# A hybrid block on one core: where half of a convolution is computed, and how attention's operands are split

## The chip, the cores and the metric

The kernel runs on one core of one Trainium2 chip. The metric is the time of one execution on the device in microseconds (us), the median of several runs. The engines go by the profile's names: PE is TensorE's matmul side and PEld its weight loads, DVE is VectorE, ACT is ScalarE, POOL is GpSimd, SP is SyncE, which here issues nearly all DMAs.

## The reference

One decoder layer for 1024 positions of 1024 channels in float32. Of it, what matters here:

```
h = rmsnorm(x);  proj = h @ w_in             # 13320 columns, split into branches
(ml_q.. ml_f, sc_b, sc_c, sc_u, sb_q, sb_k, sb_v, g_ml, g_sc, g_sb) = split(proj)
y_ml = mLSTM mixer of ml_*                   # 4 heads of 256
y_sc = sc_b * causal_conv3(sc_c * sc_u)      # per channel, 1024 channels
# stick-breaking attention, 16 heads of 64, strictly causal:
z = q k^T / 8;  a[t,s] = sigmoid(z_ts) * prod_{s<j<t} (1 - sigmoid(z_tj));  y_sb = a v
merged = sum over branches of sigmoid(g) * (y @ w_proj)
x = x + merged @ w_out;  x = x + relu(rmsnorm(x) @ w_up)^2 @ w_down;  rmsnorm(x)
```

## The kernel before, in words

**Precision.** Each float32 operand is split in two: hi, the value rounded to the matmul type float32r (ScalarE), and lo, the rest (VectorE). `split` does that (L135). A product takes three matmuls, hi by hi, hi by lo and lo by hi (`mm3`, L130 to L133).

**Stages in order of time.** The norm and transpose of x (to 100 us); the mLSTM mixer (to some 530 us); attention (537 to 1275 us); the rest of the projections of h as products of seven (to 1500 us); the three branch projections; the output projection; the MLP.

**Plain projection and product of seven.** `dense_ws` (L160) computes 128 columns of h @ w_in, transposed: two halves of 512 positions, each 8 row blocks times 3 matmuls of 128 x 512, so 48. `unit` (L781) computes 256 columns for all 1024 positions by a scheme for 2 x 2 blocks with seven products instead of eight: 7 x 4 x 3 = 84 matmuls of 128 x 512. The sums of its weight blocks are made on GpSimd (`left`, L647), and its outputs are added together on VectorE (L807).

**The convolution branch.** `sc_unit` (L693) gives three plain projections for one tile of 128 channels, and its evacuations multiply, shift and add on VectorE (L707 to L717). `conv_units` (L813) does two tiles of channels with three units. `NSC` says how many of the eight tiles go the first way; before it is 8, so the loop over `conv_units` (L836) is empty.

**Attention.** The loop over p (L748) takes 8 head pairs. `sb_v` (L497) projects v for two head pairs at once into 8 buffers, the last positions first; these are all the buffers of that kind, so the next `sb_v` waits until attention has read them. `sb_qk` (L509) projects k and q. q and k have 64 channels per head, so hi and lo of one head are stacked in 128 partitions, and two matmuls give all four products (L557, L558: one stack of q against k's stack, and against the stack with its halves swapped). Before, ScalarE and VectorE write halves of 64 partitions, and four copies by DMA (L531 to L534) fill the second halves of k's four stacks. The rings hold 6 stacks of q and 10 of k, of which a head pair uses 4 and 8.

`sb_attn` (L542) goes through blocks G of 256 queries from the last to the first, each with two heads hh. For each of two query tiles it goes through chunks of up to 512 keys from the right: scores (L557, L558), two sigmoids on ScalarE (L560, L561), masks on GpSimd for the diagonal block (L565, L567), a running product from right to left on VectorE (L573) that starts from the last value of the chunk before it (copied by L571), and a product on GpSimd (L574). The result is transposed (L591), split (L594 to L597), and multiplied with v (L604 to L608), where v's hi and lo stand side by side and so come out in the two halves of the partitions. The last diagonal block, which only the second query tile uses, has its hi and lo side by side in one matmul of 256 columns (L604) into columns 256 to 511 of the accumulator. L614 and L615 add the halves of the partitions over all 512 columns, and L618 adds the columns of that block, twice.

**What sets the order.** The order of each engine's instructions is fixed when the kernel is built: a scheduler walks through a simulated time line and lets each engine take the ready instruction with the lowest priority number, which is the order of writing. `tc.high_priority(offset=AHEAD)` puts attention 2000 places ahead, so projections fill the time that attention leaves. The projections for the convolution stand behind attention's code in each turn of the loop, three per head pair (L756), ahead of the next `sb_qk`. Two banks of PSUM (`acc`) serve all projections of this stage.

**Behind attention** the gates follow: for each of three branches, four units with a sigmoid, whose results go to DRAM (`sg_d`, L838 to L846).

Of the kernel before, what the change touches and what calls it, by code (L numbers as in the profile page):

```python
# [16 lines left out]
P = 128  # L17
# [15 lines left out]
N_RAW, N_HI, N_LO, N_SM = 2, 5, 5, 160  # L33
GROUPS = ((0, 1), (2, 3), (4, 5, 6, 7))
AHEAD = 2000
NSC = 8


@with_exitstack
def hybrid_block_kernel(  # L40
# [66 lines left out]
    def g(name):  # L107
        return rings[name].get()
# [5 lines left out]
    def unplan(base, *names):  # L114
        base.absorb(*[rings.pop(n) for n in names])
# [9 lines left out]
    def f32(ap):  # L125
        return ap.bitcast(F32)
# [382 lines left out]
    def sb_qk(p):  # L509
        Q = [[None, None], [None, None]]  # L510
        T = [[None, None] for _ in range(4)]

        def ev_q(th, ps):
            a, b = g("Q"), g("Q")
            A, B = slice(0, 64), slice(64, 128)
            r = slice(0, 512)
            nc.scalar.activation(a[A, r], ps[A, :], AF.Copy)
            nc.scalar.activation(b[B, r], ps[B, :], AF.Copy)
            nc.vector.tensor_tensor(a[B, r], ps[A, :], f32(a[A, r]), ALU.subtract)
            nc.vector.tensor_tensor(b[A, r], ps[B, :], f32(b[B, r]), ALU.subtract)  # L520
            Q[0][th], Q[1][th] = a, b

        def ev_k(th, ps):
            t1, t2, t3, t4 = [g("T") for i in range(4)]
            A, B = slice(0, 64), slice(64, 128)
            r = slice(0, 512)
            nc.scalar.activation(t1[A, r], ps[A, :], AF.Copy)
            nc.scalar.activation(t2[B, r], ps[B, :], AF.Copy)
            nc.vector.tensor_tensor(t3[A, r], ps[A, :], f32(t1[A, r]), ALU.subtract)
            nc.vector.tensor_tensor(t4[B, r], ps[B, :], f32(t2[B, r]), ALU.subtract)  # L530
            nc.sync.dma_start(f32(t1[B, r]), f32(t3[A, r]))  # L531
            nc.sync.dma_start(f32(t3[B, r]), f32(t1[A, r]))
            nc.sync.dma_start(f32(t2[A, r]), f32(t4[B, r]))
            nc.sync.dma_start(f32(t4[A, r]), f32(t2[B, r]))  # L534
            for i, t in enumerate((t1, t2, t3, t4)):
                T[i][th] = t

        dense_ws(w_in, C_SBK + p * P, hT, ev_k)
        dense_ws(w_in, C_SBQ + p * P, hT, ev_q)
        return Q, T  # L540

    def sb_attn(p, Q, T, vt):  # L542
        for G in range(3, -1, -1):
            yo = g("yo")
            for hh in range(2):
                kx, ky = (T[0], T[2]) if hh == 0 else (T[1], T[3])
                ga = {}
                for ti in (1, 0):
                    Tt = 2 * G + ti
                    qs = Q[hh][Tt // 4][:, (Tt % 4) * P:(Tt % 4 + 1) * P]  # L550
                    n = (Tt + 1) * P
                    nch = (n + 511) // 512
                    prev = None
                    for ch in range(nch - 1, -1, -1):
                        w = min(512, n - ch * 512)
                        ps = g("z")
                        mm(ps[:, :w], qs, kx[ch][:, :w], start=True, stop=False)  # L557
                        mm(ps[:, :w], qs, ky[ch][:, :w], start=False, stop=True)  # L558
                        u, be = g("u"), g("be")
                        nc.scalar.activation(u[:, :w], ps[:, :w], AF.Sigmoid, scale=-0.125)  # L560
                        nc.scalar.activation(be[:, :w], ps[:, :w], AF.Sigmoid, scale=0.125)  # L561
                        free(ps)
                        if prev is None:
                            dg = slice(w - P, w)
                            nc.gpsimd.affine_select(out=u[:, dg], in_=u[:, dg], compare_op=ALU.is_gt, fill=1.0,  # L565
                                                    base=0, pattern=[[-1, P]], channel_multiplier=1)
                            nc.gpsimd.affine_select(out=be[:, dg], in_=be[:, dg], compare_op=ALU.is_gt, fill=0.0,  # L567
                                                    base=0, pattern=[[-1, P]], channel_multiplier=1)
                            nc.gpsimd.memset(u[:, w:w + 1], 1.0)
                        else:  # L570
                            nc.gpsimd.tensor_copy(u[:, w:w + 1], prev[:, 0:1])  # L571
                        ur = u[:, 0:w][:, ::-1]
                        nc.vector.tensor_tensor_scan(ur, ur, ur, u[:, w:w + 1], ALU.mult, ALU.bypass)  # L573
                        nc.gpsimd.tensor_tensor(be[:, :w], be[:, :w], u[:, 1:w + 1], ALU.mult)  # L574
                        if prev is not None:
                            free(prev)
                        prev = u
                        ga[ti, ch] = be
                    free(prev)
                pav = g("av")  # L580
                ns = 2 * G + 2
                last = 1 if G else 0
                for s2 in range(G, -1, -1):
                    pt = g("tp")
                    for k in (0, 1):
                        s = 2 * s2 + k
                        for ti in (0, 1):
                            if s == ns - 1 and ti == 0:
                                continue
                            blk = ga[ti, s // 4][:, (s % 4) * P:(s % 4 + 1) * P]  # L590
                            nc.tensor.transpose(pt[:, k * 256 + ti * P:k * 256 + (ti + 1) * P], blk, ident)  # L591
                    ah, al = g("ah"), g("ah")
                    if s2 == G:
                        split(ah[:, 0:256], al[:, 0:256], pt[:, 0:256])  # L594
                        split(ah[:, 256:384], ah[:, 384:512], pt[:, 384:512])
                    else:
                        split(ah[:, 0:512], al[:, 0:512], pt)  # L597
                    free(pt)
                    for k in ((1, 0) if s2 == G else (0, 1)):
                        s = 2 * s2 + k  # L600
                        hd = 2 * (p % 2) + hh
                        vs = vt[s][:, hd * P:(hd + 1) * P]
                        if s == ns - 1:
                            mm(pav[:, 256:512], vs, ah[:, 256:512], start=True, stop=True)  # L604
                            continue
                        o = slice(k * 256, (k + 1) * 256)
                        mm(pav[:, 0:256], vs, ah[:, o], start=(s == ns - 2), stop=False)  # L607
                        mm(pav[:, 0:256], vs, al[:, o], start=False, stop=(s == last))  # L608
                    free(ah, al)
                free(*ga.values())  # L610
                tmp = g("avt")
                hi_r = slice(0, 64) if hh == 0 else slice(64, 128)
                lo_r = slice(64, 128) if hh == 0 else slice(0, 64)
                nc.scalar.activation(tmp[hi_r, 0:512], pav[lo_r, :], AF.Copy)  # L614
                nc.vector.tensor_tensor(yo[hi_r, 0:512], pav[hi_r, :], tmp[hi_r, 0:512], ALU.add)  # L615
                free(pav, tmp)
            for o in (256, 384):
                nc.vector.tensor_tensor(yo[:, 128:256], yo[:, 128:256], yo[:, o:o + P], ALU.add)  # L618
            nc.sync.dma_start(ysb_d[p][:, G * 256:(G + 1) * 256], yo[:, 0:256])
            free(yo)  # L620
            if G == 2:
                free(*[t[1] for t in Q + T])
        free(*[t[0] for t in Q + T])
# [124 lines left out]
    for p in range(8):  # L748
        if p % 2 == 0:
            vt = sb_v(p // 2)  # L750
        Q, T = sb_qk(p)
        with tc.high_priority(offset=AHEAD):
            sb_attn(p, Q, T, vt)
        if p % 2 == 1:
            free(*vt[::-1])
        for c0, ev in conv[len(conv) * p // 8:len(conv) * (p + 1) // 8]:  # L756
            dense_ws(w_in, c0, hT, ev)
    unplan(ring_r, "Q", "T", "V", "ah")
    unplan(ring_f, "u", "be", "yo", "avt", "sc")
    unplan(banks, "z", "av", "acc", "tp")  # L760
# [75 lines left out]
    for ct in range(NSC, KO, 2):  # L836
        conv_units(ct)
    for b, c0 in enumerate((C_GML, C_GSC, C_GSB)):  # L838
        for ct in range(0, KO, 2):
            sg = unit(c0 + ct * P, 0, AF.Sigmoid)  # L840
            for n, th in ((0, 0), (1, 1), (0, 1), (1, 0)):
                v = sg[n][th][:, :512]
                if (n, th) != (1, 0):
                    nc.scalar.activation(v, v, AF.Sigmoid)
                nc.sync.dma_start(sg_d[b][ct + n][th], v)
            free(*sg[0], *sg[1])  # L846
# [384 lines left out]
```

## Time and profile before

| | |
|---|---|
| median of three runs | 2516.52 us (2516.36 to 2519.3) |
| the profiled execution's own time | 2517.91 us |
| its span | 2516.2 us |
| mean granted clock of TensorE | 0.991 |
| busy, PE / DVE / ACT / POOL | 2449.4 / 1600.2 / 1166.7 / 870.8 us |
| matmuls | 12648 |
| chain of waits, share of PE | 87% |

A busy time is the union of an engine's instructions. A slice row cuts the span into 40 equal parts and gives the busy share of each in tenths. A window row gives the busy time of each engine in one stretch. Matmuls overlap in the records (one of 512 columns shows some 0.39 us while the next starts 0.23 us after it), so the rate is counted from starts. The chain of waits is followed backwards from the last instruction, each step to what released it.

### The profile page before, as it was taken

Reading aid. Unit: us, or ns where it says so; the run is one execution under the profiler, and the core shown is the slowest. Engines: PE = TensorE matmul, PEld = TensorE weight load, DVE = VectorE, ACT = ScalarE, POOL = GpSimd, SP = SyncE. Lnnn points to the kernel's source line nnn. Section 1 sums busy time; section 2 is a strip of 40 time slices with the busy share of each in tenths; the row PEclk is TensorE's granted clock in tenths of the full one; section 3 lists DMA queues with packets and bytes.
Section 4 is the critical chain, followed back from the end, with each engine's and each line's share of the span. In section 5 each row is a group of like instructions: output and inputs, shape, how many; then the busy total and the mean of one; then the engine's idle time right before and its main releaser. Section 6 shows DMA issues by size and latency. Waiting matters only on the chain.

```text
span 2516.2 us, 35640 instructions
## 1 busy us (share of the span) xinstructions
PE 2449.4 (97%) x12648; PEld 2064.5 (82%) x12648; DVE 1600.2 (64%) x2425; ACT 1166.7 (46%) x2358; POOL 870.8 (35%) x1188
## 2 busy tenths in 40 slices
PE   7999999999999999999899999999989999899998
PEld 6899998988888888988678878888868888678876
DVE  6564554667757757767853352444366777788896
ACT  5443333346546546546554451212456666643343
POOL 6500000024424434434732200000246565654563
PEclk9999999999999999999999999999999999999999
DMA  4321211122122122122243482433326665865663
GB/s 135 102 64 34 68 47 51 39 72 66 32 72 66 35 70 65 35 74 70 86 147 101 126 275 79 132 93 106 132 80 201 205 201 185 279 236 190 232 208 127
DMA packets 295914, 290.26 MB, mean 115 GB/s; under 512 B 22832, under 2 KB 227632, under 8 KB 295736
## 3 DMA queue, kind: packets, MB, share of 16 engines
q1 hardware_dynamic: 293288, 283.53, 36.1%
q10 hardware_dynamic: 2448, 4.46, 0.5%
q8 instruction: 99, 1.62, 0.3%
q14 instruction: 79, 0.65, 0.1%
HBM read 195.63 MB, written 83.90 MB: 111 GB/s over the span
## 4 chain that ended last, share of the span: by engine, by line
PE 87%; DVE 5%; POOL 3%; issue 2%; ACT 2%; DMA 2%; SPq 0%; POOLq 0%; ACTq 0%; DVEq 0%
PE ps L131 27%; PE ps L132 27%; PE ps L133 26%; PE ps L591 2%; DVE gr L138 2%; PE ps L558 1%; PE ps L557 1%; PE ps L608 1%; PE ps L607 1%; POOL gf L645 1%; DVE gf L573 1%; POOL gf L574 1%; DVE gf L1186 1%; DMA gf<-in_x_dram 0%; DVE wl L138 0%
## 5 line engine op out<-in xcount | busy, mean ns | idle before, releaser
L131 PE MATMUL ps<-gr,wh 128*128 128x512 f32 x1674 | 666.2, 398 | 15.1 <-ACT gf L1044 6.7
L132 PE MATMUL ps<-gr,wh 128*128 128x512 f32 x1674 | 663.6, 397 | 0.0
L133 PE MATMUL ps<-gr,wl 128*128 128x512 f32 x1652 | 653.3, 397 | 0.0
L131 PEld LDWEIGHTS ps<-gr,wh 128*128 128x128 f32 x1674 | 316.2, 189 | 88.4 <-ACT gf L1044 7.2
L132 PEld LDWEIGHTS ps<-gr,wh 128*128 128x128 f32 x1674 | 316.0, 189 | 72.2 <-DVE gr L138 0.6
L133 PEld LDWEIGHTS ps<-gr,wl 128*128 128x128 f32 x1652 | 311.3, 188 | 71.3 <-DVE wl L1126 0.3
L131 PE MATMUL ps<-gr,gr 128*128 128x512 f32 (+3 forms) x874 | 316.6, 368 | 5.2 <-DVE gf L1186 4.6
L133 PE MATMUL ps<-gr,gr 128*128 128x512 f32 (+3 forms) x874 | 318.7, 368 | 1.9 <-DVE gr L1126 1.0
L132 PE MATMUL ps<-gr,gr 128*128 128x512 f32 (+3 forms) x874 | 320.3, 368 | 0.0
L138 DVE TENSOR_TENSOR gr<-gf,gr 128x512 fp32r<-128x512 f32 (+2 forms) x250 | 229.7, 927 | 85.6 <-ACT gr L137 81.2
L137 ACT ACTIVATE wh<-wr 128x512 fp32r<-128x512 f32 (+1 forms) x226 | 142.0, 632 | 299.9 <-PE ps L132 263.5
L645 POOL TENSOR_TENSOR gf<-gf,gf 128x512 f32<-128x512 f32 x146 | 208.0, 1431 | 199.0 <-ACT gf L1058 90.3
L573 DVE TENSOR_TENSOR_SCAN gf<-gf 128x512 f32<-128x512 f32 (+1 forms) x192 | 202.3, 1056 | 95.5 <-POOL gf L565 53.8
L138 DVE TENSOR_TENSOR wl<-wr,wh 128x512 fp32r<-128x512 f32 (+1 forms) x216 | 160.0, 747 | 140.3 <-ACT wh L137 135.7
L574 POOL TENSOR_TENSOR gf<-gf,gf 128x512 f32<-128x512 f32 (+1 forms) x192 | 187.1, 977 | 170.3 <-DVE gf L573 136.5
L137 ACT ACTIVATE gr<-gf 128x512 fp32r<-128x512 f32 (+2 forms) x250 | 153.6, 623 | 180.5 <-POOL gf L645 70.0
L131 PE MATMUL ps<-wh,gr 128*128 128x256 f32 (+2 forms) x792 | 230.2, 291 | 6.7 <-DVE gf L1186 4.1
L132 PE MATMUL ps<-wl,gr 128*128 128x256 f32 (+2 forms) x800 | 229.9, 288 | 0.0
L133 PE MATMUL ps<-wh,gr 128*128 128x256 f32 (+2 forms) x792 | 226.2, 289 | 0.2 <-DVE gr L141 0.2
L137 ACT ACTIVATE gr<-ps 128x256 fp32r<-128x256 f32 (+2 forms) x304 | 129.7, 441 | 170.8 <-PE ps L133 70.7
L131 PEld LDWEIGHTS ps<-gr,gr 128*128 128x128 f32 x874 | 164.4, 188 | 38.5 <-DVE gf L1186 6.0
L133 PEld LDWEIGHTS ps<-gr,gr 128*128 128x128 f32 x874 | 164.8, 189 | 31.6 <-DVE gr L1126 1.4
(212 smaller groups left out, 4256.1 us busy)
## 6 DMA issues: line engine op xcount, KB each, us to landing
wr<-in_w_in_dram SPq DMA_DIRECT2D x78, 512.0 KB, 3.7
gr<-gd SPq DMA_DIRECT2D x145, 256.0 KB, 5.0
gd<-gr SPq DMA_DIRECT2D x128, 256.0 KB, 2.5
wr<-in_w_down_dram SPq DMA_DIRECT2D x30, 512.0 KB, 3.5
sg<-gf SPq DMA_DIRECT2D x48, 256.0 KB, 3.1
gf<-sg SPq DMA_DIRECT2D x48, 256.0 KB, 2.6
gd<-gf SPq DMA_DIRECT2D x48, 256.0 KB, 2.5
gf<-in_w_up_dram SPq DMA_DIRECT2D x36, 256.0 KB, 2.9
```

The costliest lines, as they stand in the source:

```text
L131: mm(ps, lh, rh, start=start, stop=False, skip_group_check=chain)
L132: mm(ps, lh, rl, start=False, stop=False, skip_group_check=chain)
L133: mm(ps, ll, rh, start=False, stop=stop, skip_group_check=chain)
L137: nc.scalar.activation(hi, src, AF.Copy)
L138: nc.vector.tensor_tensor(lo, src, f32(hi), ALU.subtract)
L557: mm(ps[:, :w], qs, kx[ch][:, :w], start=True, stop=False)
L558: mm(ps[:, :w], qs, ky[ch][:, :w], start=False, stop=True)
L573: nc.vector.tensor_tensor_scan(ur, ur, ur, u[:, w:w + 1], ALU.mult, ALU.bypass)
L574: nc.gpsimd.tensor_tensor(be[:, :w], be[:, :w], u[:, 1:w + 1], ALU.mult)
L591: nc.tensor.transpose(pt[:, k * 256 + ti * P:k * 256 + (ti + 1) * P], blk, ident)
L607: mm(pav[:, 0:256], vs, ah[:, o], start=(s == ns - 2), stop=False)
L645: nc.gpsimd.tensor_tensor(dst[:, :512], a[:, :512], b[:, :512], op)
```

## The change

`NSC` goes from 8 to 4: half of the convolution's channel tiles are computed by `conv_units` behind attention, with three units for each two tiles. The first two column tiles of the first branch's gate become plain projections, written behind the loop over head pairs, and their unit goes.

In `sb_qk` the evacuations split all 128 partitions at once, and copies by DMA put the halves in their places: three per half of q, which also borrows a third buffer, and six per half of k. In `sb_attn` the last diagonal block is added in place, as two matmuls of 128 columns into columns 128 to 255 of the accumulator, behind the block before it. L614 and L615 then cover 256 columns, and the two additions of L618 go.

```diff
-NSC = 8
+NSC = 4
...
+        A, B, r = slice(0, 64), slice(64, 128), slice(0, 512)
+        def cp(dst, src):
+            nc.sync.dma_start(f32(dst), f32(src))
         def ev_q(th, ps):
-            a, b = g("Q"), g("Q")
-            nc.scalar.activation(a[A, r], ps[A, :], AF.Copy)
-            nc.scalar.activation(b[B, r], ps[B, :], AF.Copy)
-            nc.vector.tensor_tensor(a[B, r], ps[A, :], f32(a[A, r]), ALU.subtract)
-            nc.vector.tensor_tensor(b[A, r], ps[B, :], f32(b[B, r]), ALU.subtract)
+            a, b, lo = g("Q"), g("Q"), g("Q")
+            split(a[:, r], lo[:, r], ps)
+            cp(b[B, r], lo[B, r])
+            cp(b[A, r], a[B, r])
+            cp(a[B, r], lo[A, r])
+            free(lo)
         def ev_k(th, ps):
             t1, t2, t3, t4 = [g("T") for i in range(4)]
-            nc.scalar.activation(t1[A, r], ps[A, :], AF.Copy)
-            nc.scalar.activation(t2[B, r], ps[B, :], AF.Copy)
-            nc.vector.tensor_tensor(t3[A, r], ps[A, :], f32(t1[A, r]), ALU.subtract)
-            nc.vector.tensor_tensor(t4[B, r], ps[B, :], f32(t2[B, r]), ALU.subtract)
-            nc.sync.dma_start(f32(t1[B, r]), f32(t3[A, r]))
-            nc.sync.dma_start(f32(t3[B, r]), f32(t1[A, r]))
-            nc.sync.dma_start(f32(t2[A, r]), f32(t4[B, r]))
-            nc.sync.dma_start(f32(t4[A, r]), f32(t2[B, r]))
+            split(t1[:, r], t3[:, r], ps)
+            for s, d in ((t1, t2), (t3, t4)):
+                cp(d[A, r], s[B, r])
+                cp(d[B, r], s[B, r])
+            for s in (t1, t3):
+                cp(s[B, r], s[A, r])
...
-                    for k in ((1, 0) if s2 == G else (0, 1)):
+                    for k in (0, 1):
                         if s == ns - 1:
-                            mm(pav[:, 256:512], vs, ah[:, 256:512], start=True, stop=True)
+                            mm(pav[:, 128:256], vs, ah[:, 256:384], start=False, stop=False)
+                            mm(pav[:, 128:256], vs, ah[:, 384:512], start=False, stop=(G == 0))
                             continue
...
-                nc.scalar.activation(tmp[hi_r, 0:512], pav[lo_r, :], AF.Copy)
-                nc.vector.tensor_tensor(yo[hi_r, 0:512], pav[hi_r, :], tmp[hi_r, 0:512], ALU.add)
+                nc.scalar.activation(tmp[hi_r, 0:256], pav[lo_r, 0:256], AF.Copy)
+                nc.vector.tensor_tensor(yo[hi_r, 0:256], pav[hi_r, 0:256], tmp[hi_r, 0:256], ALU.add)
-            for o in (256, 384):
-                nc.vector.tensor_tensor(yo[:, 128:256], yo[:, 128:256], yo[:, o:o + P], ALU.add)
...
+    for ct in range(2):
+        def ev_g(th, ps):
+            t = g("sc")
+            nc.scalar.activation(t[:, :512], ps, AF.Sigmoid)
+            nc.sync.dma_start(sg_d[0][ct][th], t[:, :512])
+            free(t)
+        dense_ws(w_in, C_GML + ct * P, hT, ev_g)
...
-        for ct in range(0, KO, 2):
+        for ct in range(2 if b == 0 else 0, KO, 2):
             sg = unit(c0 + ct * P, 0, AF.Sigmoid)
```

## Rows read from the trace of the kernel before

**Rows 1.** The page: busy time by engine, and PE's busy tenths in 40 slices.
```profile
PE 2449.4 (97%) x12648; PEld 2064.5 (82%) x12648; DVE 1600.2 (64%) x2425; ACT 1166.7 (46%) x2358; POOL 870.8 (35%) x1188
PE   7999999999999999999899999999989999899998
```

**Rows 2.** Windows: stretch, its length, busy us (x starts) PE, PEld, DVE, ACT, POOL; clock.
```profile
540.00:658.00 118.00, 118.00 (x629) 100.28 (x628) 94.16 (x135) 69.45 (x153) 61.34 (x131) 1.00 0.19 52
658.00:722.00 64.00, 62.89 (x410) 56.48 (x409) 38.05 (x69) 28.66 (x65) 15.68 (x34) 1.00 0.26 71
1220.00:1280.00 60.00, 48.84 (x226) 38.57 (x225) 47.59 (x73) 36.79 (x79) 36.06 (x41) 0.91 0.45 132
1300.00:1350.00 50.00, 50.00 (x217) 40.48 (x216) 20.32 (x27) 22.32 (x38) 14.06 (x10) 1.00 0.38 112
1500.00:1550.00 50.00, 50.00 (x217) 40.42 (x217) 14.10 (x22) 6.36 (x11) 0.00 (x0) 1.00 0.23 65
```

**Rows 3.** The chain of waits from 644 to 672 us: start, length, what.
```profile
644.17 0.66 DVE gf L707
...
650.43 1.30 DVE gf L573
...
651.89 1.09 POOL gf L574
...
671.63 0.39 PE ps L608
```

**Rows 4.** Waits of PE, 530 to 1090 us: total us, times, longest.
```profile
PE ps L608 <- DVE gr L138: 3.0, 3, 1.0
```

**Rows 5.** Timeline of DVE and ACT: start, length; head pairs 0 and 1.
```profile
540.33 1.28 DVE L573 TENSOR_TENSOR_SCAN gf<-gf 128x512 f32<-128x512 f32 x1 [5.37 <-POOL gf L565]
...
604.68 0.48 DVE L573 TENSOR_TENSOR_SCAN gf<-gf 128x128 f32<-128x128 f32 x1
...
617.20 1.28 DVE L573 TENSOR_TENSOR_SCAN gf<-gf 128x512 f32<-128x512 f32 x1 [2.42 <-POOL gf L565]
...
658.52 0.59 ACT L614 ACTIVATE gf<-ps 64x512 f32<-64x512 f32 x1 [1.38 <-PE ps L608]
```

**Rows 6.** Timeline of PE: matmuls of 128 and of 256 columns.
```profile
109.50 0.27 PE L132 MATMUL ps<-gr,gr 128*128 128x128 f32 x1
109.61 0.27 PE L133 MATMUL ps<-gr,gr 128*128 128x128 f32 x1
...
602.40 0.28 PE L608 MATMUL ps<-gr,gr 128*128 128x256 f32 x1
602.52 0.28 PE L607 MATMUL ps<-gr,gr 128*128 128x256 f32 x1
```

**Rows 7.** Groups of instructions: count, busy us, mean ns, idle before (attention's ring).
```profile
L573 DVE TENSOR_TENSOR_SCAN gf<-gf 128x512 f32<-128x512 f32 (+1 forms) x192 | 202.3, 1056 | 95.5 <-POOL gf L565 53.8
L574 POOL TENSOR_TENSOR gf<-gf,gf 128x512 f32<-128x512 f32 (+1 forms) x192 | 187.1, 977 | 170.3 <-DVE gf L573 136.5
...
L565 POOL TENSOR_SCALAR_AFFINE_SELECT gf<-gf 128x128 f32<-128x128 f32 x128 | 58.1, 454 | 232.7 <-ACT gf L560 230.8 <-PE ps L133 1.6
L571 POOL COPY gf<-gf 128x1 f32<-128x1 f32 x64 | 14.9, 233 | 0.0
```

**Rows 8.** Groups by form: the evacuations that change, and a full one.
```profile
L138 DVE TENSOR_TENSOR gr<-ps,gr 128x512 fp32r<-128x512 f32 x112 | 74.5, 677 | 33.2 <-ACT gr L137 32.7
L615 DVE TENSOR_TENSOR gf<-ps,gf 64x512 f32<-64x512 f32 x64 | 43.8, 685 | 15.2 <-ACT gf L614 14.3
L618 DVE TENSOR_TENSOR gf<-gf 128x128 f32<-128x128 f32 x64 | 21.3, 333 | 0.3
L519 DVE TENSOR_TENSOR gr<-ps,gr 64x512 fp32r<-64x512 f32 x16 | 10.9, 684 | 20.0 <-ACT gr L518 20.0
```

**Rows 9.** A stack copy's line: time on SP (ns, min/median/max), and landing.
```profile
L531 SPq DMA_DIRECT2D gr<-gr x16: 461/462/493, 516.6 to 1160.6; - x16
...
DMA to landing us min/median/max: 2.2/2.2/2.3
```

More of the change, by code (lines that the diff above doesn't have):

```diff
@@ L511, in sb_qk @@
         T = [[None, None] for _ in range(4)]
+        A, B, r = slice(0, 64), slice(64, 128), slice(0, 512)
+        def cp(dst, src):
+            nc.sync.dma_start(f32(dst), f32(src))
         def ev_q(th, ps):
-            a, b = g("Q"), g("Q")
-            A, B = slice(0, 64), slice(64, 128)
-            r = slice(0, 512)
-            nc.scalar.activation(a[A, r], ps[A, :], AF.Copy)
-            nc.scalar.activation(b[B, r], ps[B, :], AF.Copy)
-            nc.vector.tensor_tensor(a[B, r], ps[A, :], f32(a[A, r]), ALU.subtract)
-            nc.vector.tensor_tensor(b[A, r], ps[B, :], f32(b[B, r]), ALU.subtract)
+            a, b, lo = g("Q"), g("Q"), g("Q")
[4 more added lines that the diff above has]
+            free(lo)
             Q[0][th], Q[1][th] = a, b
@@ L524, in ev_k @@
             t1, t2, t3, t4 = [g("T") for i in range(4)]
-            A, B = slice(0, 64), slice(64, 128)
-            r = slice(0, 512)
-            nc.scalar.activation(t1[A, r], ps[A, :], AF.Copy)
-            nc.scalar.activation(t2[B, r], ps[B, :], AF.Copy)
-            nc.vector.tensor_tensor(t3[A, r], ps[A, :], f32(t1[A, r]), ALU.subtract)
-            nc.vector.tensor_tensor(t4[B, r], ps[B, :], f32(t2[B, r]), ALU.subtract)
-            nc.sync.dma_start(f32(t1[B, r]), f32(t3[A, r]))
-            nc.sync.dma_start(f32(t3[B, r]), f32(t1[A, r]))
-            nc.sync.dma_start(f32(t2[A, r]), f32(t4[B, r]))
-            nc.sync.dma_start(f32(t4[A, r]), f32(t2[B, r]))
+            split(t1[:, r], t3[:, r], ps)
[4 more added lines that the diff above has]
+                cp(s[B, r], s[A, r])
             for i, t in enumerate((t1, t2, t3, t4)):
@@ L581, in sb_attn @@
                 ns = 2 * G + 2
-                last = 1 if G else 0
                 for s2 in range(G, -1, -1):
@@ L607, in sb_attn @@
                         mm(pav[:, 0:256], vs, ah[:, o], start=(s == ns - 2), stop=False)
-                        mm(pav[:, 0:256], vs, al[:, o], start=False, stop=(s == last))
+                        mm(pav[:, 0:256], vs, al[:, o], start=False, stop=(s == 1))
                     free(ah, al)
```

## The prediction, made before the changed kernel was run

> **What bounds the kernel now.** The page's first part comes first: TensorE (PE) is busy 97% of the span, and its row of slices is 9 nearly everywhere [rows 1]. So a change in TensorE's work is worth its full time wherever nothing else sets the pace, and an edit that opens gaps costs their full length. The edits sit in two stages: the attention stage (537 to 1275 us) and the stage of products of seven behind it (to 1500 us). I asked for the windows of both. In the attention stage the picture repeats four times, once for each two head pairs: a burst of 118 us in which both head pairs' scans run (540 to 658), and a stretch of 64 us (658 to 722) in which the next v, k and q are projected [rows 2]. TensorE is full in the burst and lacks 1.1 us in the stretch; VectorE is busy 94.2 of 118 us, 80% [rows 2]. The last burst ends without filler: between 1220 and 1280 TensorE has 48.84 of 60 us and the granted clock falls to 0.91 [rows 2].
>
> Then the chain of waits. It is TensorE in most of the burst, but from 644 to 672 us it leaves TensorE: scan, product on GpSimd, scan, product, one after the other, until the matmul L608 takes over [rows 3]. The waits of TensorE show the join: L608 waits three times for L138, 1 us each [rows 4], one for each of the first three bursts. So the filler matmuls and attention's own chain end at nearly the same time. That decides this case: attention's chain is hidden under filler, with almost nothing to spare.
>
> **Part 1: twelve convolution projections leave the attention stage.** With NSC at 4 there are 12 plain projections beside attention, not 24. One takes 48 matmuls of 512 columns. In a stretch of plain projections 217 start in 50 us, 230.4 ns each [rows 2], so 11.06 us each: 12 x 11.06 = 132.7 us leave. Behind attention come 6 units of 84 matmuls at the same 230.4 ns (217 in 50 us among the units [rows 2]): 116.1 us. The units' other engines are far from full there (DVE 20.3, ACT 22.3, POOL 14.1 of 50 [rows 2]), so the added units should run at TensorE's pace. Work alone: -16.6 us.
>
> **Part 2: two gates plain.** One unit (84 matmuls, 19.4 us) becomes two plain projections (96, 22.1 us): +2.8 us. They come behind the last head pair without priority, so they are filler for the last burst.
>
> **Part 3: the last diagonal block.** For each of 64 (head pair, G, head) one matmul of 256 columns becomes two of 128. Starts of 256-column matmuls lie 0.12 us apart, those of 128-column ones 0.11 [rows 6]: half the columns save next to nothing. 64 x (2 x 0.11 - 0.12) = +6.4 us. From below it could cost nothing, if the second load of the same weights hid completely; I take the row. The Trainium skill (TensorE: Matmul & The Clock Gate, Back-to-back issue gap) gives about 81 ns for a 128-column matmul in a stream with weight loads; an estimate by that page is 64 x (2 x 81 - 120) = +2.7 us instead of +6.4. The row is for this data type and decides. In return VectorE loses L618 (21.3 us in all, 2.7 per head pair) and the second half of L615's columns (0.685 us each [rows 8]; as an estimate a third of it, since 512 columns take 677 ns in L138 and 128 take 333 in L618, 0.9 ns a column: 2 us per head pair).
>
> **Part 4: full splits of q and k.** Per head pair VectorE issues eight halves of 684 ns now and four full ones of 677 then [rows 8]: 2.7 us less, ScalarE alike. For that SP issues more copies: 6 rather than 4 for each half of k, 3 rather than none for each half of q. Each holds SP 0.46 us and lands 2.2 us after issue [rows 9]. The q copies form a chain: the first moves a's lower half away, and the second may only then write there. So q is ready about 0.46 + 2 x 2.2 = 5 us after the split, where now it is ready at once. Weight loads (L148) queue behind these copies on SP, but a load has 11 us of matmuls to hide behind, and one half's copies hold SP 9 x 0.46 = 4.1 us plus a wait of 2.2. The buffers matter too. A q split now borrows a third tile from a ring of six, so the second half's low part takes a tile that the previous head pair reads in its last score matmul. k's second half already waits for those matmuls today. Head pairs therefore still follow one another; they don't overlap.
>
> **Part 5: what the missing filler uncovers.** This is the largest term, and no row shows it directly. It needs the pace of attention's chain without TensorE's pressure. Per head pair, scans take 202.3 / 8 = 25.3 us, products 23.4, masks L565 7.3, copies L571 1.9 [rows 7]. On GpSimd the product of one tile stands ahead of the mask of the next, so these run one after another: 57.8 us. Measured from the first scan to the last of head pair 0: 604.7 - 540.3 = 64.4 us [rows 5]. So the pace is nearly that of the serial ring between VectorE and GpSimd, and only about 6.6 us of it is pressure from other work. With 7 us less of VectorE work per head pair from parts 3 and 4, and half the convolution's, I take 60.
>
> The burst then, from the first scan to the point where v's buffers come free (second L614 of head pair 1, 658.5 us): now 64.4 + 12.5 (handover) + 41.3 = 118.2 us [rows 5]. After: 60, a handover of 8 (split 0.7, copies 5, scores, sigmoid and mask 2), and 39 = 107. TensorE's work in it: 118 less three projections (33.2) plus part 3's 1.2 = 86. It may also run two blocks of v ahead (two accumulators; 48 matmuls of 256 columns at 0.12: 5.7 us). Idle: 107 - 86 - 5.7 = 15 us. The bounds: 0, if the chain shrinks to what TensorE has; 33 + 5, if neither the chain nor the handover gains anything and the copies' 5 us come on top. I take 15 for each of three bursts, 45 us. The fourth keeps 22 us of filler through the gates, so it loses only 11 us net against before, and the chain shortens by as much: 0.
>
> **Sum.** -16.6 + 2.8 + 6.4 + 45 = +37.6 us on the profiled execution's own 2517.9, so 2555.5; that execution lies 1.4 us above the median shown, so 2554.
>
> **The rivals.**
> Rival A: TensorE stays full. If the ring between GpSimd and VectorE is slow only because scores and transposes arrive late behind filler, attention speeds up by as much as the filler shrinks, and all saved matmul time counts: -16.6 + 2.8 + 6.4 = -7.4, and up to 10 more from waits that go (three of 1 us, and part of the 11 us at 1220). Time 2499 to 2510. For it: the chain of waits lies on TensorE for most of the burst, so filler does delay attention there, and VectorE loses 7 us of work per head pair. Against it: the chain's 28 us of scans and products [rows 3], in which TensorE isn't a link.
> Rival B: attention keeps its pace exactly. Then all 33.2 us per burst turn into idle time and the copies add 5: 3 x 38 = 115, time 2516.5 - 7.4 + 115 = 2624; with the fourth burst unharmed and some v work pulled ahead (3 x 5.7) 2607. For it: the serial sum of 57.8. Against it: convolution steps stand between scans in the chain's VectorE queue, and half of them go.
> Rival C: the gain and the idle time cancel: 2 to 3 us of idle per burst, 2512 to 2521.
>
> **How the numbers follow.** My forecast, idle of 5 to 25 us per burst: 0.47 (2525 to 2585). Rival A 0.31, B 0.12, C 0.10. The likeliest's own range is 2525 to 2585; the range that holds 8 in 10 has to take in most of A and the lower part of B: 2500 to 2600. A measurement of this kernel can tell about 0.2% (5 us) from no change. Slower by more: forecast, B, and a third of C: 0.61. Within: 0.07. Faster: 0.32.
>
> **What the changed profile would show.** Right: in the windows of the burst, TensorE at 85 to 90% with waits of L607, L608 or L557 for VectorE, ScalarE or a copy; first scan to last of a head pair still near 60 us; the distance from burst to burst (118 + 64 = 182 us by the windows now) down by 10 to 25, not by 33. The unit stage should begin earlier by some 60 us and last 116 - 19 = 97 us longer, at 217 matmuls in 50 us. Two 128-column matmuls start 0.11 us apart. q's copies land in a chain of 5 us. Wrong: TensorE at 99% in the bursts (then rival A), or scan spans that shrink to 50 us or less, which would say that the ring was held up by matmuls all along; or units slower than 19.4 us each.

## The result and the profile after

The changed kernel takes 2556.48 us (median of 4 runs, 2552.5 to 2557.05) against 2516.83 for the kernel before beside it: a ratio of 1.0156 [1.0144, 1.0168], 39 us slower. 2554 was forecast, from a sum of +37.6. The profiled execution is the lowest of the four, 2552.5 with a span of 2550.8 (before: 2517.91 and 2516.2), so the profiles have 34.6 us to explain. The mean granted clock of TensorE is 0.991 in both, so the clock explains none of them. Line numbers moved: scores are now L559 and L560, the mask L567, copies of a column L573, scans L575, products L576, transposes L592, the diagonal matmuls L605 and L606, attention's other products L609 and L610, its last evacuation L616 and L617.

The page after: busy time, TensorE's slices, the chain by engine.

```profile
PE 2456.5 (96%) x12652; PEld 2064.7 (81%) x12652; DVE 1595.1 (63%) x2351; ACT 1150.3 (45%) x2354; POOL 937.8 (37%) x1216
...
PE   7999999999998998998999999999989999999998
...
PE 82%; DVE 7%; POOL 4%; issue 3%; ACT 2%; DMA 2%; SPq 0%; POOLq 0%; DVEq 0%; ACTq 0%
```

TensorE looks nearly as full as before [rows 1]: three slices of the attention stage have turned from 9 to 8, and the one that was 8 before, where the last burst ended, is 9. Its busy time even rose by 7.1 us, though its work fell. A busy share can't show this loss; the windows by stage do. First burst, the stretch behind it, the end of the last burst, the units, in the columns of [rows 2]:

```profile
540.00:648.00 108.00, 99.45 (x574) 85.17 (x573) 87.30 (x115) 63.35 (x148) 75.58 (x140) 0.98 0.21 56
648.00:710.00 62.00, 59.62 (x354) 51.58 (x353) 25.82 (x50) 23.20 (x56) 9.29 (x23) 1.00 0.32 81
1150.00:1210.00 60.00, 51.92 (x261) 43.19 (x259) 47.61 (x65) 36.45 (x84) 44.38 (x58) 0.89 0.42 125
1300.00:1350.00 50.00, 50.00 (x217) 40.43 (x216) 24.87 (x33) 20.04 (x34) 17.68 (x13) 1.00 0.37 106
```

The burst is 10 us shorter than before [rows 2]. Its gaps by the records are 108 - 99.45 = 8.6 us, but a matmul that stands alone is drawn longer than its share of a stream, so starts say more. These are groups of the burst by form (count, then busy us and mean ns): one of three alike that hold the matmuls of 512 columns of the plain projections, before

```profile
L131 PE MATMUL ps<-gr,wh 128*128 128x512 f32 x115 | 45.6, 397 | 0.0
```

and after, with one of three alike of v's projection, which the burst did not have before:

```profile
L131 PE MATMUL ps<-gr,wh 128*128 128x512 f32 x65 | 26.4, 406 | 0.0
...
L131 PE MATMUL ps<-wh,gr 128*128 128x256 f32 x26 | 7.8, 303 | 0.5 <-DVE gf L717 0.5
```

The three sum to 347 before and 197 after: 150 x 0.230 = 34.5 us less. v's are 75, at 0.12 each 9.0 us. The diagonal adds 0.5 (ten pairs in this window at 0.05), and by an estimate from the starts 1.7 come with the few more of attention's matmuls that fall into the window (22 pairs of scores of 512 columns and not 20, most of all). That makes 118 - 34.5 + 9.0 + 0.5 + 1.7 = 94.7 us of work in 108: 13.3 us idle. The waits of TensorE, 540 to 1200 us, are now these (total us, times, longest):

```profile
PE ps L610 <- DVE gr L138: 13.4, 17, 3.5
PE ps L606 <- DVE gr L138: 10.1, 4, 2.6
PE ps L592 <- DVE gr L138: 7.5, 13, 1.2
PE ps L131 <- DVE gr L138: 3.6, 6, 0.9
PE ps L592 <- POOL gf L576: 2.5, 4, 0.6
PE ps L609 <- ACT gr L137: 2.4, 5, 0.6
PE ps L131 <- DVE gf L717: 1.6, 3, 0.5
PE ps L609 <- DVE gf L617: 0.5, 1, 0.5
```

Most of it is attention's own data: matmuls that wait for the split of transposed weights (L138 behind L592). Of the 41.6 us some 32 lie ahead of the last burst, where the kernel before had little over 3, three waits of L608 of 1 us each [rows 4] above all. The timeline of VectorE and ScalarE gives the burst's three parts, as in [rows 5]: first scan, last scan of head pair 0, first scan of head pair 1, v's buffers free, first scan of the next burst:

```profile
540.06 1.28 DVE L575 TENSOR_TENSOR_SCAN gf<-gf 128x512 f32<-128x512 f32 x1 [1.59 <-POOL gf L567]
...
592.15 0.52 DVE L575 TENSOR_TENSOR_SCAN gf<-gf 128x128 f32<-128x128 f32 x1
...
607.82 1.28 DVE L575 TENSOR_TENSOR_SCAN gf<-gf 128x512 f32<-128x512 f32 x1 [0.92 <-POOL gf L567]
...
648.08 0.38 ACT L616 ACTIVATE gf<-ps 64x256 f32<-64x256 f32 x1 [0.59 <-PE ps L610]
...
710.58 1.28 DVE L575 TENSOR_TENSOR_SCAN gf<-gf 128x512 f32<-128x512 f32 x1 [1.08 <-POOL gf L567]
```

The scan span is 52.1 us (before 64.4), the handover 15.7 (12.5), the odd part 40.3 (41.3): 108.0 in all, where before it was 118.2. From burst to burst it is 170.5 us; before, the next burst's first scan, which closes the period that [rows 5] open, came at:

```profile
725.97 1.28 DVE L573 TENSOR_TENSOR_SCAN gf<-gf 128x512 f32<-128x512 f32 x1 [3.98 <-POOL gf L565]
```

725.97 - 540.33 = 185.6. The period shrank by 15.1 us while 33.2 - 0.8 = 32.4 us of work left it, so 17.3 us are uncovered, that is, not won although the work went. The next two periods shrank from 187.0 to 171.0 and 171.1: 16.4 and 16.5 uncovered, 50.2 in all three.

### The profile page after: what moved, and what is told of

Its sections match the earlier page's. It is cut to its first block, busy times and chain, and to the rows that moved or that the text cites. A ratio compares the mean times of both kernels' runs of the same rounds, so it can differ in the third digit from the quotient of the medians.

```text
span 2550.8 us, 35761 instructions
## 1 busy us (share of the span) xinstructions
PE 2456.5 (96%) x12652; PEld 2064.7 (81%) x12652; DVE 1595.1 (63%) x2351; ACT 1150.3 (45%) x2354; POOL 937.8 (37%) x1216
## 4 chain that ended last, share of the span: by engine, by line
PE 82%; DVE 7%; POOL 4%; issue 3%; ACT 2%; DMA 2%; SPq 0%; POOLq 0%; DVEq 0%; ACTq 0%
PE ps L131 26%; PE ps L132 25%; PE ps L133 25%; DVE gr L138 2%; POOL gf L576 1%; DVE gf L575 1%; PE ps L592 1%; POOL gf L645 1%; PE ps L610 1%; PE ps L609 1%; PE ps L560 1%; DMA wr<-in_w_in_dram 1%; PE ps L559 1%; POOL gf L567 1%; DVE wl L138 1%
## 5 line engine op out<-in xcount | busy, mean ns | idle before, releaser
L131 PE MATMUL ps<-gr,wh 128*128 128x512 f32 x1558 | 620.4, 399 | 14.0 <-ACT gf L1051 6.7
L132 PE MATMUL ps<-gr,wh 128*128 128x512 f32 x1558 | 616.1, 396 | 0.0
L133 PE MATMUL ps<-gr,wl 128*128 128x512 f32 x1536 | 606.6, 396 | 0.0
L131 PEld LDWEIGHTS ps<-gr,wh 128*128 128x128 f32 x1558 | 293.7, 189 | 82.5 <-ACT gf L1051 7.1
L131 PE MATMUL ps<-gr,gr 128*128 128x512 f32 (+3 forms) x938 | 343.1, 371 | 4.8 <-DVE gf L1193 3.6
L132 PEld LDWEIGHTS ps<-gr,wh 128*128 128x128 f32 x1558 | 293.5, 188 | 66.9 <-DVE gr L138 0.7
L132 PE MATMUL ps<-gr,gr 128*128 128x512 f32 (+3 forms) x938 | 346.9, 371 | 0.0
L133 PE MATMUL ps<-gr,gr 128*128 128x512 f32 (+3 forms) x938 | 344.7, 371 | 1.5 <-DVE gr L138 0.9
L133 PEld LDWEIGHTS ps<-gr,wl 128*128 128x128 f32 x1536 | 289.1, 188 | 67.3
L138 DVE TENSOR_TENSOR gr<-gf,gr 128x512 fp32r<-128x512 f32 (+2 forms) x262 | 244.2, 941 | 81.3 <-ACT gr L137 77.5
L138 DVE TENSOR_TENSOR wl<-wr,wh 128x512 fp32r<-128x512 f32 (+1 forms) x196 | 151.1, 778 | 174.1 <-ACT wh L137 167.0
L575 DVE TENSOR_TENSOR_SCAN gf<-gf 128x512 f32<-128x512 f32 (+1 forms) x192 | 217.5, 1140 | 65.6 <-POOL gf L567 45.1
L137 ACT ACTIVATE gr<-ps 128x512 fp32r<-128x512 f32 (+2 forms) x336 | 150.5, 458 | 201.2 <-PE ps L133 98.6
L138 DVE TENSOR_TENSOR gr<-ps,gr 128x512 fp32r<-128x512 f32 (+2 forms) x336 | 163.0, 500 | 96.1 <-ACT gr L137 93.7
L576 POOL TENSOR_TENSOR gf<-gf,gf 128x512 f32<-128x512 f32 (+2 forms) x192 | 192.3, 1004 | 81.2 <-DVE gf L575 64.5
L131 PEld LDWEIGHTS ps<-gr,gr 128*128 128x128 f32 x938 | 177.0, 189 | 40.3 <-DVE gf L1193 5.8
```

The source lines that it names most:

```text
L131: mm(ps, lh, rh, start=start, stop=False, skip_group_check=chain)
L132: mm(ps, lh, rl, start=False, stop=False, skip_group_check=chain)
L133: mm(ps, ll, rh, start=False, stop=stop, skip_group_check=chain)
L137: nc.scalar.activation(hi, src, AF.Copy)
L138: nc.vector.tensor_tensor(lo, src, f32(hi), ALU.subtract)
```

## The experiments

Each ran beside the kernel before on its chip; where two kernels are compared across batches, their ratios are, times 2516.5.

**1. Fewer plain projections, and nothing else** (the kernel before).

```diff
-NSC = 8
+NSC = 4
```

> The kernel before with NSC at 4 and nothing else: 12 plain projections fewer beside attention, 6 units more behind it, attention's code and the gates as before. Filler theory (the missing filler uncovers attention's chain): work falls by 16.6 us, but each of three bursts idles some 20 us, since attention's VectorE work is not lightened, and the fourth lacks its 33 us of filler too and idles 10 to 20: 2570 to 2590 us, slower than the changed kernel (2556). Rival (the copies and the diagonal block are what costs): only the 16.6 us of saved work show, 2500 us.

Measured: 2588.48 us, ratio 1.0283 [1.0267, 1.0298], as expected: +71 us though 16.6 us of work went. The missing filler alone makes the kernel slower; the rest of the change wins part of it back. TensorE's waits, 540 to 1220 us:

```profile
PE ps L604 <- DVE gr L138: 29.5, 20, 2.6
PE ps L557 <- ACT gf L561: 10.7, 13, 1.7
PE ps L591 <- DVE gr L138: 9.2, 10, 1.4
```

L604 here is the old diagonal matmul of 256 columns, the first of its block. The scan span was 55.7 us, below the 60 of the forecast and below the 57.8 that the prediction had summed as a serial ring.

**2. The other edits with all the filler** (the changed kernel).

```diff
-NSC = 4
+NSC = 8
```

> The changed kernel with NSC back at 8: new splits of q and k, diagonal block in place, two gates plain, all of the convolution beside attention. Filler theory: TensorE is full again in the bursts; work is 2.8 + 6.4 us above the kernel before, less up to 10 us of waits at the end of the stage that the two gates fill: 2512 to 2526 us. Rival (copies and diagonal block cost most): the changed kernel's 2556 plus the 16.6 us of work, some 2570 us.

Measured: 2513.15, ratio 0.9979 [0.997, 0.9989], as expected. TensorE is full in the first burst:

```profile
540.00:658.00 118.00, 117.86 (x627) 100.11 (x625) 85.82 (x120) 63.31 (x144) 57.78 (x123) 1.00 0.25 64
```

So the loss hangs on the filler; the copies and the second diagonal matmul don't make it.

**3 and 4. Two further doses** (the changed kernel with `NSC = 6` and `NSC = 0`).

> The changed kernel with NSC at 6: 18 plain projections beside attention, two or three per head pair, 3 units behind it. With 24 of them the rest of the change takes 2513 us, with 12 it takes 2556. Filler theory with a threshold: idle time begins only where the filler is shorter than the chain (some 108 us per burst), so half of the step costs less than half of the 43 us: 2518 to 2530 us. Rival (loss in proportion): 2535 us.

> The changed kernel with NSC at 0: no convolution beside attention, 12 units behind it. Filler theory: the chain has little left to give once the filler is gone, so of the 132.7 us that leave the stage only 20 to 40 are saved and 116 come back behind it; the clock may fall where TensorE idles: 2630 to 2670 us, scan spans 48 to 52 us. Rival (matmuls still hold the chain up at NSC 4): scan spans below 45 us, 2560 to 2590 us.

Measured: 2523.35, ratio 1.0027 [1.0015, 1.0038], as expected; and 2622.9, ratio 1.0422 [1.0407, 1.0438], 7 us below what was expected. The four ratios against 2516.5 stand at -5.3, +6.8, +39.3 and +106.2 us for 8, 6, 4 and 0. Add back the work saved in each step (8.3, 8.3, 16.6 us; the removed projections are 66.4, 66.4, 132.7 us): 20.4, 40.8 and 83.5 us are uncovered, 31%, 61% and 63% of the filler taken. The first step is partly free, beyond the 3 to 4 us by which the interval of each ratio is uncertain. Past it, nearly two thirds of each microsecond of filler comes back as lost time, and a third is won by a faster attention. In the last step the mean granted clock fell too, from 0.991 to 0.979, so part of its loss is slower matmuls. With none left, the first burst:

```profile
540.00:640.00 100.00, 83.25 (x451) 68.71 (x450) 75.64 (x100) 61.60 (x145) 78.25 (x135) 0.88 0.15 38
```

Its scan spans are 49.4 and 47.3 us. No engine is full there and GpSimd, the busiest beside TensorE, has 78%: that is what a chain of handoffs looks like.

**5. The old splits of q and k** (the changed kernel, evacuations as before: four copies for k, none for q, and no third buffer).

```diff
-            a, b, lo = g("Q"), g("Q"), g("Q")
-            split(a[:, r], lo[:, r], ps)
-            cp(b[B, r], lo[B, r])
...
+            nc.scalar.activation(a[A, r], ps[A, :], AF.Copy)
+            nc.scalar.activation(b[B, r], ps[B, :], AF.Copy)
...
```

> The changed kernel with the splits of q and k as before (half-height instructions, 4 copies for k, none for q). It tells what the copies cost or save. In the changed kernel the pause between the scans of two head pairs is 15.7 us where I had predicted 8. If the copies' chain makes that pause, it falls to 10 or so and four bursts get 5 us shorter: 2535 to 2542 us. If the pause is TensorE working through q's last half after the accumulators come free, the old splits change nothing there and add 2.7 us of VectorE work per head pair: 2553 to 2566 us.

Measured: 2552.52, ratio 1.014 [1.0125, 1.0155]: 4 us below the changed kernel, with intervals that overlap, so a difference isn't shown. The pause between head pairs stayed at 15.7 us (595.33 to 611.06), but it is made of other parts. These are the start of the split of q's last half and the first score of head pair 1, in the changed kernel and then without the copies:

```profile
598.68 0.76 ACT L137 ACTIVATE gr<-ps 128x512 fp32r<-128x512 f32 x2
...
606.09 0.39 PE L559 MATMUL ps<-gr,gr 128*128 128x512 f32 x1
...
605.49 0.57 ACT L522 ACTIVATE gr<-ps 64x512 fp32r<-64x512 f32 x1
...
609.35 0.39 PE L562 MATMUL ps<-gr,gr 128*128 128x512 f32 x1
```

With the copies it is 7.4 us from split to scores, without them 3.9; but without them the split begins 10.2 us after the last scan and not 6.5. So the copies do lengthen one part, and TensorE's other order of work hides it here. Where all the filler is there, the pause is 17.4 us with the copies (experiment 2) and 14.9 without (experiment 12).

**6. A wider ring for q** (the changed kernel).

```diff
-    plan(ring_r, Q=6, T=10, V=8, ah=8)
+    plan(ring_r, Q=8, T=10, V=8, ah=6)
```

> The changed kernel with 8 buffers for q instead of 6, and 6 for the split attention weights instead of 8. q's second half then doesn't wait for the previous head pair's last score matmul to be read. If that wait makes the pause of 15.7 us between two head pairs' scans, the pause falls to 10 or less and the time to 2535 to 2545 us. If the pause comes from the two accumulators that k's second half holds (its stacks still wait for the last scores), nothing changes but the smaller ring: 2555 to 2565 us.

Measured: 2545.25, ratio 1.0113 [1.0098, 1.0128]: 11 us come back, net of what two buffers fewer for the split weights cost. The time lies at the upper edge of the first expectation, and the pause is 12.2 us, between the two:

```profile
593.82 0.47 DVE L575 TENSOR_TENSOR_SCAN gf<-gf 128x128 f32<-128x128 f32 x1
605.99 1.28 DVE L575 TENSOR_TENSOR_SCAN gf<-gf 128x512 f32<-128x512 f32 x1 [0.81 <-POOL gf L567]
```

That the wider ring is worth 11 us is shown; that q's third buffer makes the pause is not. Experiment 5 needs no third buffer and keeps the pause, and in the changed kernel the split of q's last half (598.68) follows the last of the half's 24 matmuls (597.77), when the buffer had long been free. What differs is when these matmuls run. The last score of head pair 0 and the first matmul of q's last half, in the changed kernel and then with the wider ring:

```profile
588.40 0.27 PE L560 MATMUL ps<-gr,gr 128*128 128x128 f32 x1
...
590.62 0.48 PE L131 MATMUL ps<-gr,wh 128*128 128x512 f32 x1
...
590.17 0.28 PE L560 MATMUL ps<-gr,gr 128*128 128x128 f32 x1
590.28 0.45 PE L131 MATMUL ps<-gr,wh 128*128 128x512 f32 x1
```

With the wider ring they follow the last score at once and run without a break, so the split starts 2.6 us after the last scan (596.43) and not 6.5. Why the scheduler orders them so, and whether the half could run still earlier, stays open.

**7. The old diagonal block** (the changed kernel).

```diff
-                    for k in (0, 1):
+                    for k in ((1, 0) if s2 == G else (0, 1)):
...
-                            mm(pav[:, 128:256], vs, ah[:, 256:384], start=False, stop=False)
-                            mm(pav[:, 128:256], vs, ah[:, 384:512], start=False, stop=(G == 0))
+                            mm(pav[:, 256:512], vs, ah[:, 256:512], start=True, stop=True)
...
+            for o in (256, 384):
+                nc.vector.tensor_tensor(yo[:, 128:256], yo[:, 128:256], yo[:, o:o + P], ALU.add)
```

> The changed kernel with the last diagonal block as before (one matmul of 256 columns, evacuation over 512 columns, two additions). TensorE's work falls by 6.4 us, VectorE's rises by some 4.7 us per head pair. Filler theory (the chain sets the pace now): matmul work is worth nothing and the heavier VectorE costs: 2556 to 2570 us. Rival (TensorE's work counts still): 2550 us.

Measured: 2601.93, ratio 1.033 [1.0312, 1.0347]: 44 us above the changed kernel, three times what was expected at most. Beside the filler no other edit is worth so much. TensorE's waits, 540 to 1240 us:

```profile
PE ps L606 <- DVE gr L138: 23.6, 16, 2.8
PE ps L593 <- DVE gr L138: 11.8, 13, 1.4
PE ps L559 <- ACT gf L563: 10.1, 6, 3.3
PE ps L610 <- DVE gr L138: 8.6, 7, 1.6
```

L606 is the old diagonal matmul. It stands first of its block and reads both parts of the second split, which comes after the first one; the matmuls behind it on TensorE need only the first. Three things are undone at once: the order, two additions on VectorE, and evacuations over 512 columns. Two runs part them.

**8. The old diagonal, issued last of all blocks** (the kernel of 7).

```diff
                         if s == ns - 1:
-                            mm(pav[:, 256:512], vs, ah[:, 256:512], start=True, stop=True)
+                            diag = vs, ah, al
                             continue
...
+                mm(pav[:, 256:512], diag[0], diag[1][:, 256:512], start=True, stop=True)
```

> The changed kernel with the old diagonal block (x4, 2602 us), but its one matmul is issued last of its G and head instead of first. Theory order (TensorE, in order, stands at the first matmul until VectorE has both parts of the diagonal block, 7.8 us in the first burst and stretch of x4 against 2.6): the loss goes, 2556 to 2568 us. Theory evacuation (512 columns and two additions per G on VectorE cost): it stays, 2592 to 2605 us.

Measured: 2577.05, ratio 1.024 [1.0223, 1.0257]: 23 of the 44 us go, between the two expectations. The run also holds the block's two buffers of split weights until the end of the head, which no other run does. L606's place at the head of the list is taken by L610, attention's ordinary matmul:

```profile
PE ps L610 <- DVE gr L138: 21.8, 23, 2.9
PE ps L593 <- DVE gr L138: 14.3, 14, 3.7
```

**9. Two additions more** (the changed kernel, with two additions of 128 columns into columns that nothing reads, where L618 stood).

```diff
+            for o in (256, 384):
+                nc.vector.tensor_tensor(yo[:, o:o + P], yo[:, 128:256], yo[:, 0:P], ALU.add)
```

> The changed kernel with two additions of 128 columns per G on VectorE that nobody needs (into columns that are not stored), like those that L618 did: 21 us of VectorE work in all. Theory evacuation: a large part of x4's 46 us, 2570 us or more. Theory order: 2.7 us per head pair of VectorE work in a chain that VectorE shares: 2556 to 2566 us.

Measured: 2564.34, ratio 1.019 [1.0175, 1.0205], as the theory of order expected: +8.6 us for 21.3 us of VectorE work [rows 8]. So, if the parts simply add, about 23 us of the 44 are order and about 9 the additions. The 12 left would be the wider evacuations (L614 and L615) and the buffers that experiment 8 holds longer; no run has either by itself.

**10 and 11. The gates**: as a unit again in the changed kernel, and plain in the kernel before.

```diff
-    for ct in range(2):
-        def ev_g(th, ps):
...
-        dense_ws(w_in, C_GML + ct * P, hT, ev_g)
...
-        for ct in range(2 if b == 0 else 0, KO, 2):
+        for ct in range(0, KO, 2):
```

> The changed kernel without the two plain gates: the first gate's unit is back behind attention. Work falls by 2.8 us. Filler theory: the last burst lacks 22 us of filler and idles 10 to 20 us more: 2563 to 2575 us. Rival (the last burst has filler enough, or the units behind it fill in): 2554 us.

> The kernel before with the two plain gates and nothing else. 2.8 us more work, and 22 us of filler for the last burst, where TensorE idles 11 us and runs at the lower clock for some matmuls: 2508 to 2514 us. Rival (the end of the stage is bound by attention's chain whatever stands beside it): 2519 us.

Measured: 2570.06, ratio 1.0212 [1.0197, 1.0227], 14 us worse without the plain gates; and 2506.38 (5 runs, 2505.47 to 2506.43), ratio 0.9961 [0.9947, 0.9975], 10 us better than the kernel before and a little better than expected, though the gates add 2.8 us of work. In the window that was the last burst's hole, where TensorE had 48.84 us at a clock of 0.91 [rows 2], there is now:

```profile
1220.00:1280.00 60.00, 58.32 (x296) 47.93 (x295) 46.59 (x74) 36.68 (x78) 33.46 (x45) 1.00 0.51 145
```

**12. All the filler, plain gates, the diagonal in place, old splits of q and k** (the changed kernel with `NSC = 8` and the edit of 5).

> NSC at 8, gates plain, diagonal block in place, but q and k split as before: the version that the runs so far point to. Against x2 (2513 us) the copies' chain of 5 us goes from each of four starts, at most; TensorE is nearly full there, so little of it shows: 2506 to 2513 us.

Measured: 2507.66, ratio 0.9965 [0.9952, 0.9978]. By the ratios, beside all the filler the gates are worth -9.8 us, the diagonal in place +1 and the copies +3.5; for the last two the intervals overlap, so only their smallness is shown. The kernel before with two plain gates is the fastest version measured, ahead of this one by less than the intervals tell.

## Why the prediction was right, and which of its steps were not

**The cause is as forecast.** Attention's chain was hidden under filler with almost nothing to spare, and taking half the convolution's filler uncovers it: experiments 1, 2, 3 and 4 show it by taking the filler alone, restoring it alone, and changing its dose. Which handoff of the chain costs how much, they don't part. Idle time per burst was put at 15 us and is 13.3; uncovered per period are 16.4 to 17.3. The projections of v that run ahead were put at 5.7 us and are 9.0.

**Work moved (part 1): right.** The units run at 217 matmuls in 50 us, the same as before [rows 2]. The last evacuation of attention began at 1273.29 us before and begins at 1209.25, 64.0 earlier ("some 60"); behind it stand 97 us more of units. 97 - 64 = 33 of the profile's 34.6.

**The fourth burst (parts 2 and 5) gained instead of coming to nothing.** The stage lost 132.7 - 22.1 - 3.2 = 107.4 us of work and ended 64.0 earlier: 43.4 uncovered. The first three periods alone make 50.2, so the last burst gave back about 7. It fits the gates' worth of 10 to 14 us in experiments 10 and 11: there, filler at the end of the chain is worth more than its own work costs.

**The scan span was wrong: 60 forecast, 52.1 measured.** The prediction took scans, products, masks and copies as one serial ring of 57.8 us and left 6.6 us for all other pressure. The ring is not serial. In the changed kernel the same sum, from these groups, is (217.5 + 192.3 + 58.5 + 21.1) / 8 = 61.2 us a head pair, more than the 52.1 it is said to take:

```profile
L575 DVE TENSOR_TENSOR_SCAN gf<-gf 128x512 f32<-128x512 f32 (+1 forms) x192 | 217.5, 1140 | 65.6 <-POOL gf L567 45.1
L576 POOL TENSOR_TENSOR gf<-gf,gf 128x512 f32<-128x512 f32 (+2 forms) x192 | 192.3, 1004 | 81.2 <-DVE gf L575 64.5
...
L567 POOL TENSOR_SCALAR_AFFINE_SELECT gf<-gf 128x128 f32<-128x128 f32 x128 | 58.5, 457 | 214.8 <-ACT gf L562 214.5
L573 POOL COPY gf<-gf 128x1 f32<-128x1 f32 x64 | 21.1, 333 | 2.6 <-DVE gf L575 2.6
```

So scans and products of different tiles overlap, and more than 6.6 of the 64.4 us were other work in the way: with less filler and nothing else the span is 55.7 (experiment 1), with all the filler and the rest of the change 65.1 (experiment 2). The rows could have warned: in the stretch of [rows 3] scans and products are 46% of the chain from 648 to 673 us, and steps of the convolution on VectorE are links in it. Whether the filler's matmuls or its VectorE steps held the ring up more, no run tells. The prediction had named 50 or less as the mark of a ring held up by matmuls all along; 52.1 lies close to it, and 49.4 and 47.3 without any convolution there pass it. Rival A had this half of the mechanism right.

**The handover was wrong the other way: 8 forecast, 15.7 measured.** The prediction began its count at q's split. From that split on VectorE (599.42) to the first scores it is 6.7 us, near the 5.7 of split and copies in the forecast, and 1.7 more to the scan, near its 2; the 7.3 us between the last scan and the split, in which q's last half is still being multiplied, were left out. The two errors, -8 and +8, cancel in the burst's 107 against 108.0.

**The diagonal (part 3) was priced as work and is a matter of place.** Where its two matmuls stand together without a wait, they start some 58 and 113 ns ahead of what follows (9 of the 20 pairs that stand together; one here, on TensorE's timeline):

```profile
751.37 0.22 PE L605 MATMUL ps<-gr,gr 128*128 128x128 f32 x1
751.43 0.28 PE L606 MATMUL ps<-gr,gr 128*128 128x128 f32 x1
751.54 0.34 PE L609 MATMUL ps<-gr,gr 128*128 128x256 f32 x1
```

That is 0.17 us a pair against 0.12 [rows 6], +3.2 us in all and not +6.4. The Trainium skill (TensorE: Matmul & The Clock Gate, Back-to-back issue gap) gives about 81 ns for one of 128 columns in a stream with weight loads, from which +2.7 was estimated; the trace agrees better with it than with the rows that were taken. Either is small beside 44 us, its worth once the chain sets the pace (experiment 7). Beside all the filler its worth can't be told from nothing (experiment 12).

**The copies (part 4): right as a delay, small in the total.** Each holds SP 0.46 us and lands after 2.2 to 4.2, and from split to scores they add 3.5 us (experiment 5). With and without them the totals lie 4 us apart here and 3.5 beside all the filler, both within the intervals.

**TensorE's share** in the burst was put at 85 to 90%: by the records 92%, by starts 94.7 / 108 = 88%. Of the waits named, L610's (L608 before) came, and first; behind it stand the diagonal and the transposes, not the scores.

**The rivals.** A (TensorE stays full) falls with 13.3 us idle a burst. B (attention keeps its pace) falls with a period 15.1 us shorter. C would have needed 2 to 3 us of idle a burst; with 18 of the 24 projections left (experiment 3) the kernel still comes out near it.

**How much was luck.** By these figures the sum is -16.6 + 2.8 + 3.2 + 50.2 - 7 = 32.6 of the profile's 34.6 us; the forecast had 6.4, 45 and 0 for the last three terms. The mechanism is the one forecast, but the total came out so close because errors of 3 to 8 us, in the terms and within the burst, cancelled.

## What to carry to other kernels

Before moving work away from beside a latency chain to save some of it, ask how much of it the chain needs as cover: a chain that ends within a microsecond of its filler has little cover to spare, and here each microsecond taken beyond the first step came back as 0.6 us of lost time. Small edits have two prices, one while filler hides the chain (the diagonal: nothing that can be measured) and one when it doesn't (44 us); price them in the state that the rest of the change leaves. The cheap gain was the opposite move: two plain projections put where the last burst had no filler, 10 us for 2.8 us of added work.

## What the runs showed of the hardware

- Scans, products and column copies took 1140, 1004 and 333 ns in the changed kernel and 1056, 977 and 233 before [rows 7], in the same counts, with GpSimd 70% busy in the burst and not 52%. The Trainium skill (GPSIMD Engine Reference, 1. Specifications) says that GpSimd shares its SBUF interfaces with VectorE and contends with some of its instructions; the direction agrees, and no run here separates that from waits inside an instruction.
- A burst with gaps costs clock too: 0.98 in the first burst and 0.89 at the end of the last (1.00 and 0.91 before [rows 2]), 0.88 without any convolution there; where the gates fill the end of the last burst it is 1.00. These are means of stretches in which TensorE ran partly at 1.2 and otherwise at 2.4 GHz.
